# Attention scores of 1024 keys: two full products and two of 64 rows for four full products

## The chip, the core and the metric

The kernel runs on one core of one Trainium2 chip. The metric is the device time of one execution in microseconds. The kernel before took 2750.39 us in the median of 3 runs (2749.82 to 2752.03).

## The reference

A trunk of two layers over 1024 latent tokens and 256 context tokens, model width 1024. Layer 0 mixes tokens by a Fourier transform, layer 1 by differential attention with 8 heads; each is followed by a gated feed-forward block. The change touches only the scores of the attention in layer 1:

```
def diff_attn_core(q, k, v, lam):
    s = jnp.einsum('bqhcd,bkhcd->bhcqk', q.astype(jnp.float32), k.astype(jnp.float32)) * DIFF_HEAD_DIM ** -0.5
    p = jax.nn.softmax(s, axis=-1)
    w = p[:, :, 0] - lam * p[:, :, 1]
    return jnp.einsum('bhqk,bkhe->bqhe', w, v.astype(jnp.float32)).astype(v.dtype)
```

Index `c` runs over the two softmax maps of a head; `d`, the size that is summed over, is 64. There are 1024 queries and 1280 keys (1024 latent, then 256 of the context).

## The kernel before, in words

Everything is in float32, and a product that needs the precision is built from parts: a number is split into a high part (type float32r) and a low rest. Elsewhere in the kernel a product is three (high by high, high by low, low by high; `mm3`, L49 to L52). For Q and K of the attention the two parts of 64 numbers each are stacked on the 128 rows that TensorE sums over: the K tile of one head and map holds the high part in rows 0 to 63 and the low part in rows 64 to 127. Q is held twice: `qs[:, c, 0]` in the same stacking, and `qs[:, c, 1]` with the halves exchanged (L938 to L940, three transfers). So `qs[:, c, 0]` against K gives high by high plus low by low, and `qs[:, c, 1]` against K gives the two crossed terms. `scores` (L1014) issues both into one accumulator (L1015, L1016).

The attention runs over 8 heads, each in two passes of 512 queries: 16 groups. A group has 4 blocks of 128 queries, and each block has two units, one per map: 128 units. A unit (`unit`, L1018) computes the 1024 latent scores of its block into two banks of the tile `sc`, 512 columns each. The first unit of a block also computes the 256 context scores of both maps into the tile `ct`. VectorE then moves the scores out of `sc` and `ct` into a tile `e` and finds the extreme on the way (L1029, L1030), ScalarE takes the exponential (L1031), and `combine` joins the two maps on VectorE, ScalarE and GpSimd (L1042 to L1051). The weights so made are transposed by TensorE (L1208, tile `pt`), split by ScalarE and VectorE (tile `wt`), and multiplied by V in three products (L1212 to L1214, tile `po`).

The order on TensorE is that of the program, which mixes units of later groups into the transposes and products with V of the present one (`advance`), and the builder reorders it further. So the products of one unit aren't always neighbours. `load_k` (L928) brings the two K tiles of a head, each by one transfer on SP's queue; two tiles of each name are held.

One other place matters for the reading: `ada_pe` (L239), in layer 0, multiplies with a stationary operand of 128 rows by 32 columns and writes four such products to four groups of 32 rows of one bank.

Of the kernel before, what the change touches and what calls it, by code (L numbers as in the profile page):

```python
# [20 lines left out]
P = 128  # L21
D = 1024
NC = D // P
L = 1024
LC = 256
T = L + LC
# [3 lines left out]
HD = 64  # L30
# [5 lines left out]
def trunk(tc, a, dbg=None, stop=99):  # L36
    nc = tc.nc
    V, S, G, PE = nc.vector, nc.scalar, nc.gpsimd, nc.tensor
# [7 lines left out]
    def r32(ap):  # L46
        return ap.bitcast(F32)
# [136 lines left out]
    for n, i in enumerate(PAIRS):  # L184
# [4 lines left out]
        if n % 2:  # L189
            j = n // 2  # L190
# [625 lines left out]
    kD = dram.tile([2 * H, P, T], F32, name="kD")  # L816
# [109 lines left out]
    heads, queries = {}, {}  # L926

    def load_k(h):  # L928
        heads[h] = [[kq.tile([P, T], F32R, name=f"k{c}") for c in range(2)]]
        for c in range(2):  # L930
            nc.sync.dma_start(r32(heads[h][0][c]), kD[2 * h + c])

    def load_q(h, qg):
        qsl = slice(qg * 512, (qg + 1) * 512)
        qs = kq.tile([P, 2, 2, 512], F32R, name="q")
        for c in range(2):
            src = qD[2 * h + c, :, qsl]
            nc.sync.dma_start(r32(qs[:, c, 0]), src)  # L938
            nc.sync.dma_start(r32(qs[0:HD, c, 1]), src[HD:P])
            nc.sync.dma_start(r32(qs[HD:P, c, 1]), src[0:HD])  # L940
        queries[h, qg] = qs

    for t in range(10):
        v_tile(t, 5, ws)
        if t == 2:
            flush()
            ph3.close()
            phq = ExitStack()
            kq = phq.enter_context(tc.tile_pool(name="kq", bufs=2, side="right", reuse_waits="tile"))
            load_k(0)  # L950
            load_q(0, 0)
# [40 lines left out]
    def load_v(h):  # L992
        vs = ap.tile([P, 2, 10, P], F32R, name="v")
        for s in range(2):
            nc.sync.dma_start(r32(vs[:, s]), vD[s, :, h * P:(h + 1) * P].rearrange("(t p) e -> p t e", p=P))
        heads[h].append(vs)
# [3 lines left out]
    def qk_units(h, qg):  # L1000

        if (h, qg) not in queries:
            if qg == 0:
                load_k(h)
            load_q(h, qg)
        if qg == 0:
            load_v(h)
        ks, qs = heads[h][0], queries[h, qg]
        st = ap.tile([P, 16, 4], F32, name="st", bufs=6)
        wts = [None] * 4  # L1010
        es_ = {}
        ct = {}

        def scores(out, c, jsl, ksl):  # L1014
            PE.matmul(out, qs[:, c, 0, jsl], ks[c][:, ksl], start=True, stop=False)  # L1015
            PE.matmul(out, qs[:, c, 1, jsl], ks[c][:, ksl], start=False, stop=True)  # L1016

        def unit(j, c):  # L1018
            jsl = slice(j * P, (j + 1) * P)
            col = lambda i: st[:, i, j:j + 1]  # L1020
            sc = pss.tile([P, 2, 512], F32, name="sc")
            for bk in range(2):
                scores(sc[:, bk], c, jsl, slice(bk * 512, (bk + 1) * 512))
            if c == 0:
                ct[j] = pst.tile([P, 2, LC], F32, name="ct", bufs=1)
                for cc in range(2):
                    scores(ct[j][:, cc], cc, jsl, slice(L, T))
            e = ap.tile([P, T], F32, name=f"e{c}", bufs=NE[c])
            V.tensor_scalar(e[:, 0:L], sc.rearrange("p a b -> p (a b)"), -1.0, 3.0e38, op0=ALU.mult, op1=ALU.min, accum_out=col(c))  # L1029
            V.tensor_scalar(e[:, L:T], ct[j][:, c], -1.0, col(c), op0=ALU.mult, op1=ALU.min, accum_out=col(4 + c))  # L1030
            S.activation(out=e, in_=e, func=AF.Exp, scale=-1.0, bias=col(4 + c), accum_out=col(10 + c))  # L1031
            es_[c] = e
            while comb:
                comb.pop()()
            if c == 1:
                e0, e1 = es_[0], es_[1]
                wts[j] = e0
                comb.append(lambda: combine(j, col, e0, e1))

        def combine(j, col, e0, e1):  # L1040

            V.reciprocal(col(12), col(11))  # L1042
            V.tensor_scalar(col(13), col(12), col(10), nlam, op0=ALU.mult, op1=ALU.mult, accum_out=col(14))
            if (h, qg) == (0, 0) and j in RAMP:
                V.scalar_tensor_tensor(out=e0, in0=e1, scalar=col(14), in1=e0, op0=ALU.mult, op1=ALU.add)
                return
            if j in POOLM:
                G.tensor_tensor(out=e1, in0=e1, in1=col(14).broadcast_to([P, T]), op=ALU.mult)
            else:
                S.activation(out=e1, in_=e1, func=AF.Copy, scale=col(14))  # L1050
            G.tensor_tensor(out=e0, in0=e0, in1=e1, op=ALU.add)  # L1051

        return [lambda j=j, c=c: unit(j, c) for j in range(4) for c in range(2)], st, wts

    posts = {}
# [290 lines left out]
    for nn in range(NC):  # L1346
        wu, nxt = nxt, proj_units(a["diff_w_out"][0], nn + 1) if nn + 1 < NC else None
        pb = bget()
        for k in range(NC):
            ksl = slice((k % 4) * P, (k % 4 + 1) * P)  # L1350
# [241 lines left out]
    out = a["out"].rearrange("o t d -> (o t) d")  # L1592
# [124 lines left out]
```

## Time and profile before

| | |
|---|---|
| median of 3 runs | 2750.39 us |
| the profiled execution | 2754.87 us, span 2753.1 us |
| mean granted TensorE clock | 0.988 |
| TensorE busy over the span | 2658.3 us, 97% |
| VectorE, ScalarE, GpSimd | 1544.1, 1118.4, 952.1 us |
| the scores (tile `sc`) | from 1541 to 1902 us of the span |

Busy time is the union of an engine's records. A TensorE product's record ends where a model of its pipeline puts the end, so in a dense run each record overlaps the next, and the distance between starts tells what a product costs. TensorE has two rows in the profile: PE for the products and PEld for the loads of the stationary operand. "L50" is line 50 of the kernel.

### The profile page before, as it was taken

How to read it: one execution, taken by the hardware profiler on the slowest of the kernel's cores; microseconds unless marked ns; L12 is line 12 of the kernel's file. 1: busy time of each engine (PE TensorE's matmuls, PEld its weight loads, DVE VectorE, ACT ScalarE, POOL GpSimd, SP SyncE). 2: the span in 40 equal slices, each digit the busy share in tenths (PEclk: the TensorE clock that was granted, in tenths of full speed). 3: DMA queues.
4: the chain of work that ended last, by engine and by line, in shares of the span. 5: the costliest groups of instructions: out<-in, count | busy, mean ns of one | idle time of the engine just before them, and what ended most of it. 6: DMA issues, size and time to landing. Idle time of an engine off the chain costs nothing. (4 is left out here: it accounts for less than half of the span.)

```text
span 2753.1 us, 35789 instructions
## 1 busy us (share of the span) xinstructions
PE 2658.3 (97%) x13242; PEld 2185.4 (79%) x13242; DVE 1544.1 (56%) x2867; ACT 1118.4 (41%) x1954; POOL 952.1 (35%) x786
## 2 busy tenths in 40 slices
PE   6999999999999999999999899998988999999999
PEld 3678888888888888878888677787776788888887
DVE  6744535443344343485776597898458555554242
ACT  4643333323232111242444488898444333334131
POOL 4332023312121000022333287888145666651000
PEclk9999999999999999999999999999999999999999
DMA  6583122223232111133344632423243323226352
GB/s 213 190 270 100 39 62 82 88 74 95 73 96 70 39 35 43 53 105 105 115 146 144 197 105 70 123 85 100 81 137 107 103 73 88 73 85 214 103 184 88
DMA packets 288641, 292.75 MB, mean 106 GB/s; under 512 B 16313, under 2 KB 206034, under 8 KB 288466
## 3 DMA queue, kind: packets, MB, share of 16 engines
q1 hardware_dynamic: 286306, 286.79, 33.7%
q0 software_dynamic: 2160, 3.67, 0.4%
q8 instruction: 104, 1.70, 0.3%
q14 instruction: 71, 0.58, 0.1%
HBM read 236.93 MB, written 53.48 MB: 105 GB/s over the span
## 5 line engine op out<-in xcount | busy, mean ns | idle before, releaser
L50 PE MATMUL ps<-un,whl 128*128 128x512 f32 x1184 | 465.1, 394 | 1.4 <-ACT XT L602 1.2
L51 PE MATMUL ps<-un,whl 128*128 128x512 f32 x1184 | 462.1, 390 | 0.2 <-DVE un L56 0.2
L52 PE MATMUL ps<-un,whl 128*128 128x512 f32 x1184 | 461.4, 390 | 0.0
L56 DVE TENSOR_TENSOR whl<-raw,whl 128x512 fp32r<-128x512 f32 x219 | 169.7, 787 | 267.6 <-ACT whl L55 266.5
L50 PEld LDWEIGHTS ps<-un,whl 128*128 128x128 f32 x1184 | 222.7, 188 | 55.1 <-issue 3.5
L52 PEld LDWEIGHTS ps<-un,whl 128*128 128x128 f32 x1184 | 222.7, 188 | 47.1
L51 PEld LDWEIGHTS ps<-un,whl 128*128 128x128 f32 x1184 | 222.9, 188 | 45.1 <-DVE un L56 0.7
L55 ACT ACTIVATE whl<-raw 128x512 fp32r<-128x512 f32 x219 | 134.3, 627 | 243.8 <-PE ps L52 177.9
L746 DVE SCALAR_TENSOR_TENSOR XT<-ps,mods,XT 128x512 f32<-128x512 f32 (+1 forms) x264 | 170.2, 659 | 84.7 <-PE ps L52 84.7
L272 POOL TENSOR_TENSOR acc<-acc,aw 128x512 f32<-128x512 f32 x84 | 113.1, 1346 | 295.0 <-ACT acc L268 231.7
L1051 POOL TENSOR_TENSOR e<-e,e 128x1280 f32<-128x1280 f32 x62 | 183.4, 2961 | 32.1 <-ACT e L1050 29.9
L617 POOL TENSOR_TENSOR nacc<-nacc,s 128x512 f32<-128x512 f32 (+1 forms) x35 | 41.2, 1176 | 416.7 <-ACT s L616 395.2
L1031 ACT ACTIVATE e<-e,st 128x1280 f32<-128x1280 f32 x128 | 175.2, 1372 | 23.6 <-DVE e L1030 22.0
L1029 DVE TENSOR_SCALAR_CACHE_REDUCE e<-sc 128x1024 f32<-128x1024 f32 x128 | 155.3, 1219 | 28.4 <-POOL e L1051 14.1
L51 PE MATMUL ps<-u,whl 128*128 128x256 f32 x592 | 167.5, 283 | 0.0
L52 PE MATMUL ps<-u,whl 128*128 128x256 f32 x592 | 167.4, 283 | 0.0
L50 PE MATMUL ps<-u,whl 128*128 128x256 f32 x592 | 167.3, 283 | 0.0
L829 PE MATMUL ps<-whl,un 128*128 128x512 f32 x384 | 152.7, 398 | 0.0
L830 PE MATMUL ps<-whl,un 128*128 128x512 f32 x384 | 150.3, 392 | 0.9 <-DVE whl L56 0.7
L831 PE MATMUL ps<-whl,un 128*128 128x512 f32 x384 | 149.9, 391 | 0.0
L51 PE MATMUL b<-au,wu 128*128 128x512 f32 x336 | 130.9, 390 | 0.2 <-DVE au L56 0.2
L52 PE MATMUL b<-au,wu 128*128 128x512 f32 x336 | 130.8, 389 | 0.0
(447 smaller groups left out, 6380.5 us busy)
## 6 DMA issues: line engine op xcount, KB each, us to landing
aw<-in_w_ada SPq DMA_DIRECT2D x96, 256.0 KB, 2.8
raw<-in_ffn_w_in SPq DMA_DIRECT2D x88, 256.0 KB, 2.9
wr<-in_ffn_w_out SPq DMA_DIRECT2D x42, 512.0 KB, 3.6
wada<-in_w_ada SPq DMA_DIRECT2D x48, 256.0 KB, 3.2
un<-in_w_ada SPq DMA_DIRECT2D x48, 256.0 KB, 4.6
raw<-in_diff_w_in SPq DMA_DIRECT2D x48, 256.0 KB, 3.5
rq<-in_ffn_w_in SPq DMA_DIRECT2D x24, 512.0 KB, 5.7
raw<-in_ffn_w_out SPq DMA_DIRECT2D x44, 256.0 KB, 2.9
```

The costliest lines, as they stand in the source:

```text
L50: PE.matmul(out, wh, mh, start=start, stop=False)
L51: PE.matmul(out, wh, ml, start=False, stop=False)
L52: PE.matmul(out, wl, mh, start=False, stop=stop)
L55: S.activation(out=hl[:, 0], in_=src, func=AF.Copy)
L56: (lo_eng or V).tensor_tensor(out=hl[:, 1], in0=src, in1=r32(hl[:, 0]), op=ALU.subtract)
L746: V.scalar_tensor_tensor(out=xs, in0=pt, scalar=gmod[c][:, nn:nn + 1], in1=xs, op0=ALU.mult, op1=ALU.add)
L829: PE.matmul(pt, hk[:, 0, tsl], ws[k][:, 0], start=k == 0, stop=False)
L830: PE.matmul(pt, hk[:, 0, tsl], ws[k][:, 1], start=False, stop=False)
L831: PE.matmul(pt, hk[:, 1, tsl], ws[k][:, 0], start=False, stop=k == NC - 1)
L1029: V.tensor_scalar(e[:, 0:L], sc.rearrange("p a b -> p (a b)"), -1.0, 3.0e38, op0=ALU.mult, op1=ALU.min, accum_out=col(c))
L1031: S.activation(out=e, in_=e, func=AF.Exp, scale=-1.0, bias=col(4 + c), accum_out=col(10 + c))
L1051: G.tensor_tensor(out=e0, in0=e0, in1=e1, op=ALU.add)
```

## The change

The K tile is loaded in three transfers: columns 0 to 511 as before, and columns 512 to 1279 with the high and the low half exchanged. For each unit the first two products are the crossed terms of the two banks, over all 128 rows: for bank 0 the exchanged Q against K, for bank 1 the straight Q against the exchanged K. The other two are the high by high terms over 64 rows, rows 0 to 63 for bank 0 and rows 64 to 127 for bank 1. The low by low term of the 1024 latent keys is no longer computed. The context columns lie in the exchanged part of K and keep both full products.

```
     def load_k(h):
         heads[h] = [[kq.tile([P, T], F32R, name=f"k{c}") for c in range(2)]]
         for c in range(2):
-            nc.sync.dma_start(r32(heads[h][0][c]), kD[2 * h + c])
+            kt, src = r32(heads[h][0][c]), kD[2 * h + c]
+            nc.sync.dma_start(kt[:, 0:512], src[:, 0:512])
+            nc.sync.dma_start(kt[0:HD, 512:T], src[HD:P, 512:T])
+            nc.sync.dma_start(kt[HD:P, 512:T], src[0:HD, 512:T])
...
-        def scores(out, c, jsl, ksl):
-            PE.matmul(out, qs[:, c, 0, jsl], ks[c][:, ksl], start=True, stop=False)
-            PE.matmul(out, qs[:, c, 1, jsl], ks[c][:, ksl], start=False, stop=True)
+        def scores(jsl, *parts):
+            for out, c, ksl, low in parts:
+                PE.matmul(out, qs[:, c, 1 - low, jsl], ks[c][:, ksl], start=True, stop=False)
+            for out, c, ksl, low in parts:
+                rows = slice(HD, P) if low else slice(0, HD)
+                PE.matmul(out, qs[rows, c, low, jsl], ks[c][rows, ksl], start=False, stop=True)
...
-            for bk in range(2):
-                scores(sc[:, bk], c, jsl, slice(bk * 512, (bk + 1) * 512))
+            scores(jsl, *((sc[:, bk], c, slice(bk * 512, (bk + 1) * 512), bk) for bk in range(2)))
             if c == 0:
                 ct[j] = pst.tile([P, 2, LC], F32, name="ct", bufs=1)
                 for cc in range(2):
-                    scores(ct[j][:, cc], cc, jsl, slice(L, T))
+                    for m in range(2):
+                        PE.matmul(ct[j][:, cc], qs[:, cc, m, jsl], ks[cc][:, L:T], start=m == 0, stop=m == 1)
```

The order of the instructions on VectorE, ScalarE and GpSimd is the same in both kernels. On TensorE, in the middle of the attention, this stood before; L1015 and L1016 are the straight and the exchanged Q, `k_13738` and `k_13739` the K tiles of the two maps:

```order
L1015 MATMUL sc<-k_13738,q 128x512
L1016 MATMUL sc<-k_13738,q 128x512
L1015 MATMUL sc<-k_13738,q 128x512
L1016 MATMUL sc<-k_13738,q 128x512
L1015 MATMUL sc<-k_13739,q 128x512
L1016 MATMUL sc<-k_13739,q 128x512
L1015 MATMUL sc<-k_13739,q 128x512
L1016 MATMUL sc<-k_13739,q 128x512
L1208 MATMUL pt<-ident,e_13490 128x128
```

In the changed kernel the same place reads as follows; L1021 are the full products, L1024 those of 64 rows, L1216 the transposes, and the K tiles are called `k_13746` and `k_13747`:

```order
L1021 MATMUL sc<-k_13746,q 128x512 x2
L1024 MATMUL sc<-k_13746,q 128x512 x2
L1021 MATMUL sc<-k_13747,q 128x512 x2
L1024 MATMUL sc<-k_13747,q 128x512 x2
L1216 MATMUL pt<-ident,e_13498 128x128
```

Here the two products of 64 rows are neighbours, between full ones on either side. A few rows further on in TensorE's order of the kernel before, a unit's fourth product is set apart from its third:

```order
L1015 MATMUL sc<-k_13738,q 128x512
L1016 MATMUL sc<-k_13738,q 128x512
L1015 MATMUL sc<-k_13738,q 128x512
L1214 MATMUL po<-wt,v 128x512
L1097 MATMUL pt<-ident,on 128x128 x4
L1015 MATMUL ct<-k_13738,q 128x256
L1016 MATMUL ct<-k_13738,q 128x256
L1015 MATMUL ct<-k_13739,q 128x256
L1016 MATMUL ct<-k_13739,q 128x256
L1016 MATMUL sc<-k_13738,q 128x512
```

In the changed kernel the same unit has its two products of 64 rows in the third and the fourth place, with the same other work between them (L1222 is a product with V, L1105 transposes, L1035 the context scores):

```order
L1021 MATMUL sc<-k_13746,q 128x512 x2
L1024 MATMUL sc<-k_13746,q 128x512
L1222 MATMUL po<-wt,v 128x512
L1105 MATMUL pt<-ident,on 128x128 x4
L1035 MATMUL ct<-k_13746,q 128x256 x2
L1035 MATMUL ct<-k_13747,q 128x256 x2
L1024 MATMUL sc<-k_13746,q 128x512
```

Nothing but the kind of the four products moved: the places are the old ones.

## Rows read from the trace of the kernel before

**Rows 1.** Windows: us, busy PE, PEld, DVE, ACT, POOL; clock, DMA, GB/s.
```profile
1541.00:1580.00 39.00, 30.23 (x130) 22.30 (x129) 32.93 (x88) 24.35 (x35) 16.18 (x8) 0.87 0.65 189
1580.00:1780.00 200.00, 189.13 (x1029) 152.25 (x1028) 171.84 (x461) 171.72 (x313) 159.73 (x130) 0.97 0.36 104
1780.00:1902.00 122.00, 121.55 (x694) 100.44 (x694) 112.25 (x303) 113.59 (x206) 105.31 (x80) 1.00 0.29 82
```
**Rows 2.** Timeline of PE in a dense run: start us, length us, instruction, count.
```profile
1863.09 0.60 PE L1208 MATMUL pt<-ident,e 128*128 128x128 f32 x4
...
1863.88 0.28 PE L1016 MATMUL ct<-k,q 128*128 128x256 f32 x1
1864.00 0.40 PE L1015 MATMUL sc<-k,q 128*128 128x512 f32 x1
1864.23 0.39 PE L1016 MATMUL sc<-k,q 128*128 128x512 f32 x1
```
**Rows 3.** Windows of PE's products into `sc`: us, busy (count), clock, DMA, GB/s.
```profile
1541.00:1580.00 39.00, 20.95 (x64) 0.87 0.65 189
1580.00:1780.00 200.00, 83.42 (x271) 0.97 0.36 104
1780.00:1902.00 122.00, 52.99 (x176) 1.00 0.29 82
```
**Rows 4.** The same of PE's products into `ct`, the context scores.
```profile
1580.00:1780.00 200.00, 26.49 (x136) 0.97 0.36 104
1780.00:1902.00 122.00, 17.13 (x89) 1.00 0.29 82
```
**Rows 5.** The same of PE's products into `po`, the products with V.
```profile
1580.00:1780.00 200.00, 80.21 (x241) 0.97 0.36 104
1780.00:1902.00 122.00, 53.66 (x165) 1.00 0.29 82
```
**Rows 6.** The same of PE's transposes into `pt`.
```profile
1580.00:1780.00 200.00, 57.98 (x381) 0.97 0.36 104
1780.00:1902.00 122.00, 38.14 (x264) 1.00 0.29 82
```
**Rows 7.** Timeline of PE around eight products of L239 in layer 0.
```profile
182.02 0.39 PE L51 MATMUL ps<-un,whl 128*128 128x512 f32 x1
182.25 0.39 PE L52 MATMUL ps<-un,whl 128*128 128x512 f32 x1
182.57 1.06 PE L239 MATMUL ps<-un,cond 128*32 128x512 f32 x8
183.56 0.50 PE L50 MATMUL ps<-un,whl 128*128 128x512 f32 x1
183.90 0.39 PE L51 MATMUL ps<-un,whl 128*128 128x512 f32 x1
```
**Rows 8.** Timeline of PEld, the weight loads, in the same stretch.
```profile
182.03 0.19 PEld L52 LDWEIGHTS ps<-un,whl 128*128 128x128 f32 x1
182.57 0.16 PEld L239 LDWEIGHTS ps<-un,cond 128*32 128x32 f32 x8 [0.35 <-DMA raw<-in_fnet_w_out]
183.56 0.19 PEld L50 LDWEIGHTS ps<-un,whl 128*128 128x128 f32 x1 [0.84 <-ACT aw L271]
```
**Rows 9.** Timeline of PE at two transposes of 112 and 41 rows.
```profile
28.70 0.39 PE L52 MATMUL ps<-mo,un 128*128 128x512 f32 x1
28.94 0.26 PE L217 MATMUL ps<-ident,rows 112*128 112x112 f32 x1
29.13 0.25 PE L218 MATMUL ps<-ident,rows 41*128 41x41 f32 x1
```
**Rows 10.** Timeline of PEld at the same two.
```profile
28.71 0.14 PEld L217 LDWEIGHTS ps<-ident,rows 112*128 112x128 f32 x1
29.12 0.13 PEld L218 LDWEIGHTS ps<-ident,rows 41*128 41x128 f32 x1 [0.28 <-DMA wada<-in_w_ada]
```
**Rows 11.** DMA issues: transfer, queue, count, KB each, median us from issue to landing.
```profile
k<-kD SPq DMA_DIRECT2D x16, 640.0 KB, 6.7
```

## The prediction

> **What bounds the kernel now.** The change touches only the attention stage, so I read that stage and not the page's shares. The tile view of the scores names it: `sc` is written from 1541 to 1902 us. The windows of three stretches of it [rows 1] show four engines loaded nearly alike. In the last 122 us TensorE is busy for 121.6, ScalarE for 113.6, VectorE for 112.3 and GpSimd for 105.3; in the middle 200 us the same order stands at 189, 172, 172 and 160. So TensorE is the first bound and the others stand some 7 to 16% behind it.
>
> A busy TensorE hides small gaps, since a record's end is modelled, so I recount it by pitch, the distance from start to start in a dense run [rows 2]: 0.23 us for 512 columns, 0.12 for 256, 0.11 for a transpose (four take 0.60, one 0.27). With the counts by tile [rows 3 to 6] the last stretch holds 176 score products, 89 context products, 165 of `po` and 264 transposes: 40.5 + 10.7 + 38.0 + 29.0 = 118.2 of 122 us. That is TensorE-bound with 3% to spare. The middle stretch gives 62.3 + 16.3 + 55.4 + 41.9 = 176 of 200, so 24 us are free. In the first, the ramp, TensorE is busy for 30 of 39 us by its records.
>
> **The change part by part.** A unit (one block of queries, one of the two softmax maps, 1024 keys) has four full products before, and has two full and two of 64 rows after. All other engines run the same instructions in the same order; only TensorE's and SP's rows differ. The unit keeps its four places in TensorE's order, and there the catch lies: the order puts other work between the third and the fourth place in many units. I counted in the new order: of 128 units, 78 have the two 64-row products next to each other, and 50 have something full-height between them, which makes 100 lone ones. So TensorE is turned to 64-row products and back 178 times in this stage, and not once in it before.
>
> *What is removed.* A pair side by side costs one pass of 0.23 us in place of two if the halves really overlap: 78 x 0.22 = 17 us. A lone half saves nothing.
>
> *What is added.* The kernel before has no pair of 64-row products. The nearest rows are those of L239, where a product uses 32 of the 128 columns and four of them stand side by side between ordinary products. I take the visit at 182 us [rows 7, 8]. Its weight loads and products run four abreast (eight loads have 0.16 us of busy time together), so side by side does work. But the way in and out costs four things:
> - In: the product before starts at 182.25, and the first L239 product 0.32 later instead of 0.23: 0.09 us.
> - In: ordinarily a weight load starts together with the product before its own (182.03 beside 182.02). Here it starts with its own product (both 182.57), so it isn't hidden. A load of 128 columns, which the new halves need, shows its price at the way out: a first product of 0.50 us instead of 0.39, 0.34 from the next instead of 0.23, so 0.11 us.
> - Out: ordinarily the next product starts 0.16 us before the modelled end of the last (0.39 long, 0.23 apart). Here the last group ends at 182.57 + 1.06 = 183.63, and the next starts at 183.56, only 0.07 before: 0.09 us.
> - Out: its weight load starts with it (183.56) and isn't hidden: 0.11 us.
>
> The second row of rows 8 names a transfer as what the first load waited for, but that is inferred: the trace has 36 such visits, and at all but two, where data came late, the way in is late by the same 0.07 to 0.10 us. For halves with loads of 128 columns I add the four: 0.40 us a visit. That it holds for fewer rows, and not for fewer columns alone, rests on one place [rows 9, 10]: the transpose L217 (112 rows) has its load with the product before (28.71 beside 28.70), but L218 (41 rows) has it with itself, 0.19 after L217 where transposes stand 0.11 apart. The wait that the row names is inferred, so this is a hint and no proof.
>
> The Trainium skill, "TensorEngine Tiling (Array Packing)", section Key Properties, says that a change of tiling mode, not of the tile alone, drains the engine. That speaks against this change, and the rows of L239 bear it out for columns. The other way, "TensorE: Matmul & The Clock Gate", Part 3, gives a pack the span of one product and about 4 ns for each further tile, with no charge for coming and going; by that alone the sum would be the 17 us removed and nothing added, my first rival below.
>
> *Bounds and choice.* The extra cost of a visit lies between nothing (the loads hide, as they do between full products) and 0.40 us (L239). Below nothing it can't go, since as many columns are streamed. I take 0.40, because L239 is the only repeated row in which the kind of product changes. A pair then costs 0.40 + 0.01 - 0.23 = 0.18 more than before, a lone half 0.40 more: 78 x 0.18 + 100 x 0.40 = 14 + 40 = 54 us of TensorE time.
>
> *Where it falls.* By the order and the counts of `sc` [rows 3] the first stretch has 14 pairs and 4 lone halves (4 us), the middle 39 and 57 (30 us), the last 25 and 39 (20 us). The last has no room: all 20 are on the path. The middle has 24 us free, of which the 3% that remain even in the densest stretch (6 us) will remain; of the other 18 I let half take up the cost: 21 us. In the first TensorE waits for others: 1 us. Sum: 42 us. With all 18 taken up and the first at nothing it is 20 + 12 = 32, with none taken up 54.
>
> *The loads of K.* Each of the 16 K tiles comes by three transfers and not one, so SP issues 48 instead of 16, ahead of the loads of Q and V that follow them in its queue. The bytes are the same. One took 6.7 us from issue to landing before [rows 11], and two tiles of each name are held, so the head before, some 45 us (8 heads in 361 us), covers it. I cost it at nothing; if that cover failed in each of the 7 later heads by half a landing, 3.4 us, it would be 23 us.
>
> The context products stay four of 256 columns to a pair of units; with K's halves exchanged there they sum the same four terms. The dropped low by low product of the 1024 keys was no instruction of its own.
>
> The profiled execution took 2754.9 us, 4.5 above the median of the runs (2750.4); the difference is carried over: 2750.4 + 42 = 2792.
>
> **The rivals.**
> 1. *Halves overlap and the visits are free.* For it: L239 does run four abreast, and its eight loads lie in 0.16 us. Against: every one of its visits pays. TensorE is then eased by 5.5 us in the last stretch, 8.6 in the middle and 3 in the first. The last gains all (ScalarE at 93% would come next), the middle half, the first 1: 11 us, 2739.
> 2. *The halves neither overlap nor cost a visit* (the 64-row product is treated as any other): four passes as before, 2750. Against it stands only what speaks for the two others.
> 3. *Visits cost and the pairs don't overlap:* 78 x 0.22 = 17 us more on top, of which the same share lands on the path: 42 + 14 = 56, 2806. Against it: four abreast in rows 7 and 8.
>
> Rival 1 ends on the other side, and the price of a visit decides: with 100 lone halves among 178 visits TensorE breaks even at 17 / 178 = 0.10 us, a quarter of what I take.
>
> **How the numbers follow.** The forecast has 0.72, rival 3 0.08, rival 1 0.12, rival 2 0.08. The likeliest case's own range is 2776 to 2808. To leave out no more than 2 in 10, the range goes from 2745, which takes in rival 2, to 2812, which takes in rival 3 with a little more on the path. About 0.2% (5.5 us) is what a measurement of this kernel can tell from no change. Slower by more: 0.81; within: 0.08; faster: 0.11.
>
> **What would show it.** In the changed profile the first 64-row product should start some 0.32 us after a 512-column one, with its weight load at its own start, and the full product behind it should be 0.50 long. Two halves in a row should start some 0.01 us apart. TensorE should be busy through the middle stretch too, VectorE's and ScalarE's shares in all of it should fall to about 80%, and the last `sc` should be written about 40 us later than now, with the stages behind it as long as they are. It is wrong if loads of the halves start with the product before: then the stage gets shorter by about 10 us. If the visits cost as said and the stage still grows by less than 30, the middle's free time took more than I let it.

## The result and the profile after

The changed kernel takes 2783.29 us in the median of 4 runs (2779.60 to 2784.74), against 2751.21 for the kernel before on the same chip: 32 us more, a ratio of 1.0114 with a 95% interval of 1.0097 to 1.0132. Forecast was slower, 2792, in 2745 to 2812.

The span of the profiled execution grew by 27.0 us, from 2753.1 to 2780.1. The tile view of the scores puts all of it into the attention: `sc` is now written from 1537.5 to 1927.4 us, 390 us against 361 before; it begins 3.5 us earlier. From the last score to the end it is 853 us, much as before (851). The medians differ by 32 us and the two profiled executions by 27 (2754.87 and 2781.93); single executions of one kernel differ by as much (2779.60 to 2784.74).

What a visit to the 64-row products costs can be read directly. This is TensorE's timeline of the changed kernel around one pair; columns as in [rows 2].

```profile
1707.20 0.39 PE L1220 MATMUL po<-wt,v 128*128 128x512 f32 x1
1707.43 0.40 PE L1221 MATMUL po<-wt,v 128*128 128x512 f32 x1
1707.76 0.50 PE L1024 MATMUL sc<-k,q 64*128 64x512 f32 x2
1708.19 0.50 PE L1222 MATMUL po<-wt,v 128*128 128x512 f32 x1
1708.53 0.60 PE L1216 MATMUL pt<-ident,e 128*128 128x128 f32 x4
```

The same stretch in the weight loads:

```profile
1707.20 0.19 PEld L1221 LDWEIGHTS po<-wt,v 128*128 128x128 f32 x1
1707.76 0.18 PEld L1024 LDWEIGHTS sc<-k,q 64*128 64x128 f32 x2 [0.36 <-issue]
1708.19 0.19 PEld L1222 LDWEIGHTS po<-wt,v 128*128 128x128 f32 x1 [0.25 <-issue]
```

It is the picture of [rows 7, 8] with rows in place of columns. The pair starts 0.33 after the product before it and not 0.23; its loads start with it; the product behind it lasts 0.50 and is 0.34 ahead of the next. The two halves together have 0.50 us of busy time, as much as one alone (the lone one below), and the trace has the 78 pairs' halves 3 to 4 ns apart. From 1707.43 to 1708.53 it is 1.10 us, where three dense full products take 0.69 and four 0.92: a pair costs 0.41 more than one pass and 0.18 more than the two it replaces. Over the trace the median is 0.17 for the 78 pairs and 0.39 for the 100 lone halves, worked out from the starts on either side; that is 13 + 39 = 52 us in all. A lone one:

```profile
1868.52 0.50 PE L1024 MATMUL sc<-k,q 64*128 64x512 f32 x1
1868.95 0.50 PE L1220 MATMUL po<-wt,v 128*128 128x512 f32 x1
1869.29 0.40 PE L1221 MATMUL po<-wt,v 128*128 128x512 f32 x1
```

The windows of the stage after, cut roughly where the stretches of [rows 1] end in work done (the middle one holds 1059 products and not 1029, the last 650 and not 694); columns as there:

```profile
1537.00:1580.00 43.00, 35.79 (x146) 20.58 (x145) 36.29 (x99) 27.76 (x41) 19.78 (x9) 0.88 0.65 190
1580.00:1800.00 220.00, 216.60 (x1059) 145.77 (x1058) 177.84 (x476) 178.04 (x319) 166.43 (x135) 0.99 0.36 94
1800.00:1928.00 128.00, 127.96 (x650) 88.81 (x651) 105.22 (x279) 108.48 (x197) 96.51 (x73) 1.00 0.26 73
```

TensorE is now busy for 98% of the middle stretch, where it was 189 of 200 us; VectorE and ScalarE have fallen from 86 to 81%, GpSimd from 80 to 76%. The granted clock of that stretch rose from 0.97 to 0.99. The clock has two levels, 1.2 and 2.4 GHz, so less of the stretch ran at the lower one. What TensorE itself waited for shrank, as the waits after and then before show (engine, what for: us in total, times, longest):

```profile
PE sc L1021 <- DVE e L1037: 2.7, 4, 1.6
```

```profile
PE sc L1015 <- DVE e L1029: 10.5, 11, 3.6
```

Where the time came in, the ends of groups tell. ScalarE copies `po` once at the end of each of the 16 groups; these are the copies after groups 1, 8 and 14, first before, then after (start us, length, instruction).

```profile
1593.62 0.58 ACT L1064 ACTIVATE of<-po 128x512 f32<-128x512 f32 x1
1769.60 0.60 ACT L1064 ACTIVATE of<-po 128x512 f32<-128x512 f32 x1
1904.98 0.60 ACT L1064 ACTIVATE of<-po 128x512 f32<-128x512 f32 x1 [0.33 <-PE po L1214]
```

```profile
1591.26 0.60 ACT L1072 ACTIVATE of<-po 128x512 f32<-128x512 f32 x1 [0.69 <-PE po L1222]
1776.80 0.60 ACT L1072 ACTIVATE of<-po 128x512 f32<-128x512 f32 x1 [0.42 <-PE po L1222]
1930.44 0.60 ACT L1072 ACTIVATE of<-po 128x512 f32<-128x512 f32 x1 [0.85 <-PE po L1222]
```

Groups 2 to 8 took 176.0 us before and 185.5 after, 9.5 more; groups 9 to 14 took 135.4 and 153.6, 18.2 more. Group 1, from the first score on, grew by 1.2. Counted in the trace, of the 54 us of visits 5 fall on group 1 (4 lone halves, 20 pairs), 26 on groups 2 to 8 (51 and 32) and 23 on groups 9 to 14 (45 and 26).

### The profile page after: what moved, and what is told of

Same layout as the page of the kernel before. It is cut to its first block, busy times and chain, and to the rows that moved or that the text cites. A ratio compares the mean times of both kernels' runs of the same rounds, so it can differ in the third digit from the quotient of the medians.

```text
span 2780.1 us, 35811 instructions
## 1 busy us (share of the span) xinstructions
PE 2696.5 (97%) x13242; PEld 2163.8 (78%) x13242; DVE 1545.2 (56%) x2867; ACT 1122.7 (40%) x1954; POOL 951.3 (34%) x786
## 5 line engine op out<-in xcount | busy, mean ns | idle before, releaser
L1037 DVE TENSOR_SCALAR_CACHE_REDUCE e<-sc 128x1024 f32<-128x1024 f32 x128 | 155.3, 1219 | 37.9 <-PE pt L1216 18.2
```

## The experiments

Theory A: the visits cost TensorE 54 us, and the stage takes up a fixed stock of that in time it had free. Rivals: the new transfers of K (B), a fixed share of any cost on the path (C), harm beyond TensorE's time (D), and for single points E, F and G below. Each difference is to the runs of the kernel before on the same chip. In the first three and the last two experiments VectorE, ScalarE and GpSimd have the instruction order of both kernels; in the others the builder orders them differently.

**No 64-row product** (full_height).

```
-                rows = slice(HD, P) if low else slice(0, HD)
+                rows = slice(0, P)
```

> The changed kernel with one line different: the two high-by-high products run over all 128 rows again (K exchanged and loaded in three transfers, order of all engines as in the changed kernel). No product of 64 rows is left. Theory A (the 178 visits to 64-row products cost TensorE 54 us, of which 29 lengthen the stage): no visit, so the time of the kernel before, 2751 (2746 to 2756), stage 361 us. Rival B (the three transfers of K, or the exchanged columns, cost it): as slow as the changed kernel, 2783.

2750.78 against 2750.40 us, ratio 1.0000 (0.9991 to 1.0010). The transfers of K cost nothing, though each of the smaller ones lands in 5.5 us in the changed kernel (transfer, queue, count, KB, us to landing; before in [rows 11]):

```profile
k<-kD SPq DMA_DIRECT2D x32, 192.0 KB, 5.5
k<-kD SPq DMA_DIRECT2D x16, 256.0 KB, 2.7
```

Rival B falls: all of the 32 us hangs on the 64-row products.

**Halves ahead of the full products** (halves_first).

```
             for out, c, ksl, low in parts:
-                PE.matmul(out, qs[:, c, 1 - low, jsl], ks[c][:, ksl], start=True, stop=False)
+                rows = slice(HD, P) if low else slice(0, HD)
+                PE.matmul(out, qs[rows, c, low, jsl], ks[c][rows, ksl], start=True, stop=False)
             for out, c, ksl, low in parts:
-                rows = slice(HD, P) if low else slice(0, HD)
-                PE.matmul(out, qs[rows, c, low, jsl], ks[c][rows, ksl], start=False, stop=True)
+                PE.matmul(out, qs[:, c, 1 - low, jsl], ks[c][:, ksl], start=False, stop=True)
```

> The changed kernel with the two 64-row products issued before the two full ones of a unit. By the order of the new program 99 pairs stay neighbours and 58 halves are alone: 157 visits and not 178, and 99 x 0.18 + 58 x 0.40 = 41 us of TensorE time more than four full products, not 54; the order of the other engines is unchanged. Theory A with a fixed stock of free time (25 us taken up, the rest on the path): +16, 2767. Rival C (a fixed share of the cost, 59%, is on the path): +24, 2775. Rival B: 2783.

2777.20, 26.8 more, ratio 1.0093 (1.0077 to 1.0109). Fewer visits are cheaper, but the gain is 5 us and not 16: theory A's number is missed, C's is nearer. It isn't the price of a visit: the trace has a median of 0.17 for its 99 pairs and 0.39 for its 58 lone halves, as in the change.

**Every half alone** (halves_alone): the 64-row product stands in the first loop, behind the full product of its bank.

```
             for out, c, ksl, low in parts:
                 PE.matmul(out, qs[:, c, 1 - low, jsl], ks[c][:, ksl], start=True, stop=False)
-            for out, c, ksl, low in parts:
                 rows = slice(HD, P) if low else slice(0, HD)
```

> The changed kernel with the 64-row product of a bank right after the full product of the same bank, so every one of the 256 halves is alone: 256 visits, 256 x 0.40 = 102 us of TensorE time more. Theory A with a fixed stock of free time: +77, 2828. Rival C (59%): +60, 2811. Rival B (K's transfers): 2783.

2827.89, 77.5 more, ratio 1.0280 (1.0258 to 1.0303). Theory A's number to the microsecond; C (60) is out. That it fits so closely is partly luck: in the ramp the granted clock was lower than in the changed kernel (0.88 in the same window, above),

```profile
1537.00:1580.00 43.00, 42.53 (x92) 20.96 (x90) 26.18 (x72) 19.18 (x28) 14.33 (x7) 0.58 0.58 173
```

and group 1 alone grew by 19.4 us, more than the 18 us of its visits, while groups 2 to 8 took up more than in any other of these kernels (table below).

**Plain float32** (plain_f32).

```
-                rows = slice(HD, P) if low else slice(0, HD)
-                PE.matmul(out, qs[rows, c, low, jsl], ks[c][rows, ksl], start=False, stop=True)
+                PE.matmul(out, r32(qs[:, c, low, jsl]), r32(ks[c][:, ksl]), start=False, stop=True)
```

> All four products full, the two high-by-high ones as plain float32, which take 0.43 us and not 0.23 for 512 columns (the pitch of L239 in the trace before): 256 x 0.20 = 51 us of ordinary TensorE time, no visit. The builder orders some instructions differently. Theory A (the visits harm only by TensorE time): +26, about 2777, as the changed kernel within 8 us. Rival D (the visits harm by more than TensorE time, by waits at their ends): clearly less, under +12, 2763.

2881.06, 130.7 more: a miss by 104 us, because the dose (the TensorE time added) was not what I had worked out. TensorE's groups in the stage (line, shape, count, busy, mean ns) and a pair of records show it:

```profile
L1023 PE MATMUL sc<-k,q 128*128 128x512 f32 x511 | 249.3, 592 | 0.0
```

```profile
1803.28 1.02 PE L1023 MATMUL sc<-k,q 128*128 128x512 f32 x2
```

256 plain products leave 512 records (511 in this window), so each is two, and two records stand 1.02 - 0.59 = 0.43 apart. A product takes 0.86 us and the dose was 256 x 0.63 = 161 us. Against that 130.7 leaves 30 us taken up, but the run no longer compares equal doses.

**Ordinary passes added** (two_more_passes, one_more_pass), to the kernel before, in place of the call of `scores`:

```
...
+                PE.matmul(sc[:, bk], qs[:, c, 0, jsl], ks[c][:, ksl], start=True, stop=False)
+                if bk >= 0:    # one_more_pass: bk >= 1
+                    PE.matmul(sc[:, bk], qs[:, c, 1, jsl], ks[c][:, ksl], start=False, stop=False)
+                PE.matmul(sc[:, bk], qs[:, c, 1, jsl], ks[c][:, ksl], start=False, stop=True)
```

> The kernel before with the crossed product of each bank issued twice, so six full products in a unit and not four (the scores get a second crossed term). 256 x 0.23 = 59 us of ordinary TensorE time, no visit. The builder orders some instructions otherwise. Theory A (the stage takes up the first 14 to 25 us and the rest lengthens it, whatever the time is made of): +34 to +45, 2784 to 2796. Rival D (the visits harm the other engines beyond TensorE's time, so ordinary time does less than 54 us of visits did): under +25, below 2775.

> The kernel before with the crossed product of the second bank issued twice: five full products in a unit, 29 us of ordinary TensorE time. Theory A (a stock of 14 to 25 us is taken up first): +4 to +15, 2755 to 2766. Rival C (59% of any cost is on the path): +17, 2768.

2787.46, 35.7 more, ratio 1.0125 (1.0105 to 1.0145), and 2759.09, 7.3 more, ratio 1.0024 (1.0013 to 1.0035). Both within theory A's range. 59 us of plain streaming do what 54 us of visits do, so rival D falls: no harm of a visit beyond TensorE's time shows. A few us of it would not be seen here, since the order of the other engines and the clock differ too. And half of the dose costs a fifth, so a fixed share (C) falls again. With one more pass the middle stretch has no time free any more (columns as in [rows 1]):

```profile
1541.00:1580.00 39.00, 31.78 (x161) 24.88 (x162) 35.44 (x98) 26.32 (x40) 22.40 (x12) 1.00 0.67 206
1580.00:1780.00 200.00, 199.07 (x1109) 163.18 (x1109) 175.75 (x465) 173.85 (x316) 162.74 (x132) 1.00 0.34 97
```

The clock is 1.00 in both, where the kernel before had 0.87 and 0.97 [rows 1]. Worked out from these rows, 0.13 x 39 + 0.03 x 200 = 11 us of the 22 that the stage seems to take up can be the clock that came back, and not free time: an estimate, and an upper one, since time at the lower clock costs nothing where TensorE waits anyway. two_more_passes, empty_visits and plain_f32 have 1.00 in groups 2 to 8 too.

**Visits with nothing in them** (empty_visits): in the kernel before, between the two products of the second bank,

```
...
+                if bk == 1:
+                    PE.matmul(sc[:, 1, 0:2], qs[0:HD, c, 1, jsl], ks[c][0:HD, 512:514], start=False, stop=False)
```

> The kernel before with one 64-row product of 2 columns put into each unit between the second bank's two full products; nothing is removed. 128 visits of 0.40 to 0.43 us, 51 to 55 us of TensorE time. Theory A (the price is that of the visit, not of the 512 columns): +27 to +35, 2778 to 2786. Rival E (most of what a visit costs is the product's own columns): under +10, 2760.

2777.18, 25.4 more, ratio 1.0096 (1.0077 to 1.0116). It lies 2 us under theory A's range and far over rival E's. The timeline of one such visit:

```profile
1862.51 0.40 PE L1024 MATMUL sc<-k,q 128*128 128x512 f32 x1
1862.83 0.27 PE L1026 MATMUL sc<-k,q 64*128 64x2 f32 x1
1863.03 0.51 PE L1027 MATMUL sc<-k,q 128*128 128x512 f32 x1
1863.37 0.40 PE L1024 MATMUL sc<-k,q 128*128 128x512 f32 x1
```

0.86 us from the first to the last row, where two dense products take 0.46: the visit costs 0.40 without any columns to speak of.

**Two columns** (two_columns): the changed kernel with the two high-by-high products over all rows, as in full_height, and over 2 columns:

```
-                rows = slice(HD, P) if low else slice(0, HD)
-                PE.matmul(out, qs[rows, c, low, jsl], ks[c][rows, ksl], start=False, stop=True)
+                n = slice(ksl.start, ksl.start + 2)
+                PE.matmul(out[:, 0:2], qs[:, c, low, jsl], ks[c][:, n], start=False, stop=True)
```

> The kernel with four full products and K exchanged, in which the two high-by-high products compute 2 of their 512 columns (the rest of that term is left out). Each then costs the 0.11 us of its weight load and not 0.23: 256 x 0.12 = 31 us of TensorE time less, no visit. It bounds what a saving on TensorE can bring. Theory A (TensorE is first only in the last stretch, with ScalarE at 93% close behind): -5 to -12, 2738 to 2746. Rival F (TensorE alone bounds the stage): -25 or more, below 2726.

2774.81, 23.0 more, ratio 1.0089 (1.0071 to 1.0106): wrong for both. The builder put much of VectorE's order elsewhere for the shorter products, and TensorE now waits in the stage: 34.1 us before the full products of the scores alone, 31.0 of it for VectorE.

```profile
L1021 PE MATMUL sc<-k,q 128*128 128x512 f32 x254 | 95.5, 449 | 34.1 <-DVE e L1037 31.0 <-issue 1.9 <-PE sc L1024 0.3
```

So the run is no bound for what a saving is worth; that stays open. It shows only that another order of this stage can cost as much as the change did.

**Both halves on the same rows** (same_rows).

```
-                rows = slice(HD, P) if low else slice(0, HD)
+                rows = slice(0, HD)
```

> The changed kernel with both 64-row products on rows 0 to 63 (the second bank then gets its low-by-low term and not its high-by-high). Places and order are those of the changed kernel; neighbouring halves can no longer run side by side. Theory A: 78 x 0.23 = 18 us more TensorE time, 54 + 18 = 72 in all, less the 23 us that the stage took up in the runs so far: +49, 2800. Rival G (the neighbouring halves gain nothing by running side by side, the visit covers it): as the changed kernel, 2783.

2802.50, 50.6 more, ratio 1.0181 (1.0164 to 1.0198): theory A's 2800, and 19 us over the changed kernel. Two halves now have 0.73 us of busy time and not 0.50:

```profile
1865.04 0.73 PE L1024 MATMUL sc<-k,q 64*128 64x512 f32 x2
1865.70 0.73 PE L1021 MATMUL sc<-k,q 128*128 128x512 f32 x2
```

Rival G falls. Running side by side saves what it promises; the visit is what eats it. The parts fit less well than their sum: against the changed kernel, group 1, at a lower granted clock (0.78 and not 0.90), grew by 8 us where 5 were due, groups 2 to 8 by 5 where 7 were due, groups 9 to 14 by the 6 that were due.

**Full, half, half, full** (halves_between): the second and the third place of each unit are the 64-row products.

```
...
+            whole(*parts[0], True)
+            half(*parts[0], False)
+            half(*parts[1], True)
+            whole(*parts[1], False)
```

> The changed kernel with the order full, half, half, full in each unit. By the order of the program 91 pairs stay neighbours and 74 halves are alone: 91 x 0.18 + 74 x 0.40 = 46 us of TensorE time more, order of the other engines unchanged. Theory A with a stock of 23 us: +23, 2774. If the halves' place in the unit counts by itself, as halves_first left open (+27 for 41 us, a stock of 14): +32, 2783.

2786.30, 34.4 more, ratio 1.0126 (1.0111 to 1.0141). Fewer lone halves than in the changed kernel, and yet no faster: the number of the second theory is missed by 2 us, that of a stock of 23 by 11. With halves_first it is the second such case, and here too a pair costs 0.17 and a lone half 0.39 in the trace. Part of it is in the ramp. The windows from 1560 to 1580 us of the changed kernel and of halves_between:

```profile
1560.00:1580.00 20.00, 17.27 (x78) 10.70 (x78) 17.61 (x50) 14.25 (x22) 12.01 (x5) 0.91 0.46 149
```

```profile
1560.00:1580.00 20.00, 16.93 (x56) 10.53 (x54) 14.43 (x39) 10.16 (x15) 10.08 (x5) 0.66 0.41 136
```

TensorE's granted clock is 0.66 there and not 0.91, and group 1, from the first score on, takes 57.5 us and not 53.8. That these 4 us come from the place of the halves, and not from where the clock's fall happened to lie, wasn't tried and stays open. The other part is free time that stays free. TensorE's waits for VectorE in the stage, of halves_first and of halves_between, where the changed kernel has 2.7 us:

```profile
PE sc L1022 <- DVE e L1037: 7.8, 9, 3.2
PE sc L1021 <- DVE e L1043: 7.0, 9, 2.9
```

All doses in one table:

| kernel | TensorE time added, worked out | time added, measured | taken up |
|---|---|---|---|
| one_more_pass | 29 | 7.3 | 22 |
| halves_first | 41 | 26.8 | 14 |
| halves_between | 46 | 34.4 | 12 |
| empty_visits | 51 | 25.4 | 26 |
| the change | 54 | 32.1 | 22 |
| two_more_passes | 59 | 35.7 | 23 |
| same_rows | 72 | 50.6 | 21 |
| halves_alone | 102 | 77.5 | 25 |
| plain_f32 | 161 | 130.7 | 30 |

By these sums, beyond a stock of some 21 to 26 us each microsecond of TensorE time lengthens the kernel by one, whether it is visits or columns; the two kernels with the halves in earlier places have 10 less and plain_f32 has some more. By groups it isn't one stock. These are the growth in the profiled execution and, behind "of", the TensorE time added, both in us, for the kernels in which the other engines keep their order; the last two columns are the granted clock of group 1 and of groups 2 to 8 (0.90 and 0.97 in the kernel before).

| kernel | group 1 | groups 2 to 8 | groups 9 to 14 | clock, 1 | clock, 2 to 8 |
|---|---|---|---|---|---|
| halves_first | 5.2 of 6 | 9.2 of 21 | 11.8 of 14 | 0.85 | 0.98 |
| halves_between | 4.8 of 4 | 10.0 of 19 | 21.2 of 23 | 0.85 | 0.98 |
| the change | 1.2 of 5 | 9.5 of 26 | 18.2 of 23 | 0.90 | 0.99 |
| same_rows | 9.1 of 10 | 14.8 of 34 | 23.8 of 29 | 0.78 | 0.99 |
| halves_alone | 19.4 of 18 | 24.4 of 46 | 33.9 of 39 | 0.72 | 1.00 |

Groups 9 to 14, at a clock of 1.00 in all, put everything on the path but 2 to 5 us: this is the clean case of one for one. Groups 2 to 8 take up 9 to 22 us, the more the more is added. Group 1 takes up 4 us in the change and next to nothing in the others, whose clock was lower there; why it was lower stays open.

## Why the prediction was right

- *Side by side saves 17 us.* Right: same_rows takes it away and is 19 us slower.
- *A visit costs 0.40, a pair 0.18, a lone half 0.40 more.* Right: 0.17 and 0.39 in the trace, 0.40 for the empty visit. L239, read for columns, held for rows, and the hint of L218 [rows 9, 10] pointed the right way. The working says that all visits of L239 but two come in 0.07 to 0.10 us late; in the trace it is all but five of the 36 (three more are 0.19 to 0.20 late), which doesn't touch the price. The Trainium skill's "TensorEngine Tiling (Array Packing)", Key Properties, that a change of tiling mode drains the engine, agrees with these rows. The span that the Trainium skill's "TensorE: Matmul & The Clock Gate", Part 3, gives a pack is right for the pack itself (3 to 4 ns between the halves), but it leaves out the way in and out, which here is the larger part.
- *50 of 128 pairs are torn apart by the order.* Right, and decisive: the 100 lone halves are 40 of the 54 us.
- *54 us of TensorE time.* Right: 52 by the medians of the trace, and 59 us of ordinary passes do much the same (35.7).
- *Of these 42 on the path.* This term was mis-sized: 32.1 was measured, 29 by the stage in the trace. "Of the other 18 I let half take up the cost" is where most of it went: groups 2 to 8 grew by 9.5 of their 26 us, so they took up 17 and not 9. "The last has no room: all 20 are on the path" was nearly right: groups 9 to 14 grew by 18.2 of their 23 us, so the 3% to spare, which the working had found there and left as it was, was filled too. Group 1 took up 4 of 5, about as forecast. The bound worked out beside it, 32 with all 18 taken up, meets the 32.1 by some luck, since it gives the last stretch no room. The sign that the forecast named for this case, visits at the price said and a stage that grows by less than 30, is what came; the last score is 25 us later and not 40.
- *Why the middle took up more.* Free time of TensorE in front of waits for others is filled first: its wait for VectorE fell from 10.5 to 2.7 us. And some 3 to 4 us of the 17 can be the clock, which rose from 0.97 to 0.99 there (an estimate, 0.02 x 176 us). The working took all 24 us beyond the pitch for free time, though at 0.97 part of it was products at the lower clock.
- *The loads of K cost nothing.* Right (full_height).
- *The other shares fall to about 80%.* Right: over the 390 us VectorE is at 82% and ScalarE at 80%.

Of the rivals, 1 and 2 fall with the visit's price, 3 with the halves' 3 to 4 ns and same_rows.

## What to carry to other kernels

Products of fewer rows pay here only if several follow each other: a visit costs 0.40 us, nearly two full passes of 512 columns, and a pair saves only one. By these numbers two pairs in one visit would about break even (0.40 + 2 x 0.23 = 0.86 us against 0.92 for four full products); that is an estimate, and no run tried it. Before counting on neighbours, read the final order on the engine, since a builder that interleaves may tear them apart. And where one engine is at 90% beside others at 85%, let a cost fill that engine's free time first and put the rest on the path one for one; but work this out stretch by stretch, with the granted clock of each, since time at the lower clock looks like free time in a count by pitch.

## What was not expected of the hardware

A plain float32 product of 512 columns is two records of 0.43 us on TensorE, 0.86 in all, against 0.23 for the float32r product. So the eight records of L239 in [rows 7] are four products. And two 64-row products on the same rows take 0.23 us more than two on different rows (0.73 against 0.50 of busy time), which is the whole pass.
